# Expert tokens gathered from DRAM by indirect DMA, instead of one-hot products

## The chip, the cores and the metric

The kernel runs on one core of a Trainium2 chip. The metric is device time in microseconds (us). Before the change the median of three runs is 2654.95 us (2649.46 to 2660.77).

## The reference

Two layers of a hybrid network over 512 tokens (256 context, 256 latent; the second layer's output is needed for the latent 256 alone). Each layer has four token mixers, an output projection, a second RMSNorm and a mixture of experts. The change lies in the last two. Cut to what matters:

```python
def hier_moe(h, p):                       # h: the tokens after the second norm
    g_sel = argmax(h @ w_router_g + b_router_g)          # 1 of 4 groups
    top_v, top_i = lax.top_k(e_logits[rows, g_sel], 2)   # 2 of its 8 experts
    weights = softmax(top_v) * g_w
    ...
    # each expert: its tokens' rows, silu(rows @ w_gate) * (rows @ w_up) @ w_down,
    # added to the token with the token's weight
```

An expert has three fp32 matrices: gate and up of 1024x512, down of 512x1024. There are 32 experts in a layer, and all of their weights are read in each layer: 192 MiB. Every token goes to two of them.

## The kernel before

**The second norm.** `tail` (L1597) takes the token tiles of 128 one by one: `project` forms the output projection and adds it to the residual `x`, `norm2` (L1407) makes the normed rows `h2` on VectorE, transposes them on TensorE (8 transposes of 128x128 fp32, L1426) for the router's product, and `split3` (L1432) splits them into three bfloat16 parts whose sum is the fp32 row: the tile `h2p`, 128 partitions by 3 parts by `nt` token tiles by 1024, which stays in SBUF. `nt` is 4 in layer 0 and 2 in layer 1. ScalarE and, by turns, VectorE and GpSimd do the split. `route` (L1439) then makes, for each token and expert, its position in the expert's list (`posm`, -1 where it isn't routed there) and its weight, again as three bfloat16 parts (`wt3`).

**A pair of experts.** `moe` (L1636) goes through 16 pairs. For each, `pair` (L1524) has 128 places, 64 for either expert. `onehot` (L1517) compares `posm` with 0 to 63 on VectorE: a bfloat16 matrix of tokens by places with a 1 where a token holds a place. The expert's tokens, transposed, come from products of `h2p` with it: 8 blocks of 128 features, `nt` token tiles and 3 parts each, summed in PSUM (tile `pg`) and copied to `xT` by ScalarE. Products of the one-hot with the weights give each place's weight (`pw`, `ws`); a transpose of the one-hot (`pT`, `oT`) brings results back to tokens. Then the gate and the up product (`pgate`, `pup`: 32 matmul records each, two experts in two halves of the columns), the activation (`hd`), four transposes (`ph`), the down product (`pd`), the weighting (`yp`, two parts), and the products `py` with `oT`, which add to `x`: the left half of the features on VectorE, the right half by way of ScalarE (`ta`, three buffers) and GpSimd.

**Weights.** `eload` (L1666) brings the weights in tiles of 1 MiB, 12 for a pair in the order gate, up, down, on SyncE's queue. They go round a ring of slots: `EB` (L25) says how many lie on the left and on the right of SBUF in each layer, and four more are the buffers of the output projection's weights. That is 4 + 5 + 4 = 13 slots in layer 0 and 6 + 5 + 4 = 15 in layer 1. The left ones are opened (L1856) and filled before `tail`, the right ones (L1873) as soon as the buffers below them come free. A load into a slot waits on SyncE's queue until the product that read the slot's former tile is done.

**Order.** The kernel is written with a tile framework that lists each engine's instructions in an order of its own making when the program is built, by what it supposes to be ready; at run time each engine keeps that order. So the one-hot products of the next pair stand between the other matmuls of this one, in places that differ from pair to pair. An expert with over 64 tokens would go through `overflow` (L1701), a loop at run time that calls `pair` once more; the counts of the matmul records (1024 for `pgate`, 32 for each of 32 pairs) show that it has no turn here.

Of the kernel before, what the change touches and what calls it, by code (L numbers as in the profile page):

```python
# [9 lines left out]
F32 = mybir.dt.float32  # L10
BF = mybir.dt.bfloat16
F32R = mybir.dt.float32r
I32 = mybir.dt.int32
AF = mybir.ActivationFunctionType
OP = mybir.AluOpType
AX = mybir.AxisListType
# [4 lines left out]
D = 1024  # L21
T = 512
EPS = 1e-6
GN_EPS = 64e-5
EB = ((4, 5), (6, 5))  # L25
CDEC = math.exp(-0.5)
NEG = -1e30

# [9 lines left out]
C_SLT = C_MG + 128  # L38
C_MA = C_SLT + 128
C_ROPE = C_MA + 256  # L40
C_END = C_ROPE + 128

P_N1, P_N2, P_MU, P_W0, P_A0, P_KK, P_KA, P_RK, P_LNG = 0, 8, 16, 24, 28, 32, 34, 36, 38
P_AB, P_GLN, P_BGLU = 40, 42, 44
# [3 lines left out]
def _consts():  # L48
    c = np.zeros((128, C_END), np.float32)
    p = np.arange(128)  # L50
    c[:, C_ID:C_ID + 128] = np.eye(128)
    s = p % 64
    t = np.arange(64)
    c[:, C_MRW:C_MRW + 64] = s[:, None] < t
    c[:, C_MRW + 64:C_MRW + 128] = s[:, None] <= t
    c[:, C_MG:C_MG + 64] = s[:, None] <= t
    c[:, C_MG + 64:C_MG + 128] = s[:, None] >= t
    q = np.arange(128)
    c[:, C_MA:C_MA + 128] = np.where(q[None, :] <= p[:, None], 0.0, NEG)
    c[:, C_MA + 128:C_MA + 256] = np.where(q[None, :] >= p[:, None], 0.0, NEG)  # L60
    c[:, C_BLK:C_BLK + 128] = (p[:, None] // 64) == (p[None, :] // 64)
    tok = np.arange(256, dtype=np.float32)
    inv = np.float32(10000.0) ** (-np.arange(16, dtype=np.float32) / np.float32(16))
    ang = np.concatenate([np.floor(tok / 64)[:, None] * inv, (tok % 64)[:, None] * inv], axis=1)
    ang = ang.astype(np.float32)
    c[:, C_ROPE:C_ROPE + 64] = np.cos(ang).reshape(2, 128, 32).transpose(1, 0, 2).reshape(128, 64)
    c[:, C_ROPE + 64:C_ROPE + 128] = np.sin(ang).reshape(2, 128, 32).transpose(1, 0, 2).reshape(128, 64)

    r = p % 32
    c[:, C_SEL:C_SEL + 12 * L] = r[:, None] == np.arange(12 * L)  # L70
    c[:, C_SLT:C_SLT + 128] = p[:, None] < p[None, :]
    c[:, C_IO:C_IO + 64] = np.arange(64)

    un = p[:, None] % 4 * 4 + np.arange(4)[None, :]
    c[:, C_UN:C_UN + 64] = (un[:, :, None] == np.arange(16)).reshape(128, 64)

    c[:, C_MK:C_MK + 4] = s[:, None] // 16 == np.arange(4)
    return c
# [97 lines left out]
class Net:  # L176
# [1227 lines left out]
            self.tt(xo, xo, tm, OP.add, self.nc.gpsimd if n else None)  # L1404


    def norm2(self, t, x, rw, lo, h2p, wr, lg, pool):  # L1407

        nc = self.nc
        V, G = nc.vector, nc.gpsimd  # L1410
        s, tl = t // 2, t - lo // 128
        xs = x[t]
        y = self.rstd([xs], pool, "n2", 2)
        h2 = pool.tile([128, D], F32, tag="h2", bufs=2, name="h2")
        for n in range(2):
            self.bt = f"B{n}"
            cs = slice(512 * n, 512 * n + 512)
            self.stt(h2[:, cs], xs[:, cs], y, self.bcast(rw, 40 + s, n), OP.mult, OP.mult)
            self.tt(h2[:, cs], self.bcast(rw, 6 + s, n), h2[:, cs], OP.add)
        hT = pool.tile([128, 8, 128], F32, tag="h2T", bufs=1, name="h2T")  # L1420
        for kb in range(2):
            self.bt = f"B{kb}"
            ps = self.pb()
            for k in range(4):
                c = 512 * kb + 128 * k
                nc.tensor.transpose(ps[:, 128 * k:128 * k + 128], h2[:, c:c + 128], self.ident)  # L1426
            (V.tensor_copy if kb else nc.scalar.copy)(hT[:, 4 * kb:4 * kb + 4, :].rearrange("p k n -> p (k n)"), ps)
        for k in range(8):
            self.mm(lg[:, 36 * tl:36 * tl + 36], hT[:, k, :], wr[:, k, :], k == 0, k == 7)
        self.split3([h2p[:, i, tl, :] for i in range(3)], h2, G if t % 2 else V)  # L1430

    def split3(self, o, r, eng):  # L1432

# [87 lines left out]
                    self.cst[:, None, C_IO:C_IO + 64].to_broadcast([128, nt, 64]), OP.is_equal)  # L1521
        return p

    def pair(self, wts, posv, wtv, h2p, x, mb, lo, pool, pooled=(1, 1, 1, 1)):  # L1524

        nc = self.nc
        V, G = nc.vector, nc.gpsimd
        nt = (512 - lo) // 128
        wg, wu, wd = wts
        p = self.onehot(posv, nt, pool, "oh", 2)  # L1530
        pf = p.rearrange("p t e n -> p t (e n)")
        xT = pool.tile([128, 8, 128], F32, tag="xT", bufs=2, name="xT")
        for kb in range(2):
            ps = self.bank("G", "pg")
            for kk in range(4):
                k = 4 * kb + kk
                for t in range(nt):
                    for i in range(3):
                        self.mm(ps[:, 128 * kk:128 * kk + 128], h2p[:, i, t, 128 * k:128 * k + 128], pf[:, t, :],
                                t == 0 and i == 0, t == nt - 1 and i == 2)  # L1540
            self.act(xT[:, 4 * kb:4 * kb + 4, :].rearrange("p k n -> p (k n)"), ps, AF.Copy)
        pT = self.bank("C", "pT", BF)
        for t in range(nt):
            nc.tensor.transpose(pT[:, 128 * t:128 * t + 128], pf[:, t, :], self.identb)
        oT = pool.tile([128, nt, 128], F32R, tag="oT", bufs=2, name="oT")
        V.tensor_copy(oT.rearrange("p t n -> p (t n)"), pT[:, 0:128 * nt])
        pw = self.pc("pw")
        for t in range(nt):
            self.mm(pw[:, 0:6], pf[:, t, :], wtv[:, t], t == 0, t == nt - 1)
        ws = pool.tile([128, 1], F32, tag="ws", bufs=2, name="ws")  # L1550
        for e in range(2):
            r = slice(64 * e, 64 * e + 64)
            V.tensor_reduce(ws[r], pw[r, 3 * e:3 * e + 3], AX.X, OP.add)
        pg, pu = self.pa("pgate"), self.pa("pup")
        for ps, w in ((pg, wg), (pu, wu)):
            for k in range(8):
# [40 lines left out]
    def tail(self, l, lo, acc, rm, w):  # L1597
# [4 lines left out]
        st["posm"] = posm = rm.tile([128, nt, 32], F32, name="posm")  # L1602
        st["wt3"] = wt3 = rm.tile([128, nt, 32, 3], BF, name="wt3")
        st["cnt"] = cnt = rm.tile([128, 32], F32, name="cnt")
        st["h2p"] = h2p = rm.tile([128, 3, nt, D], BF, name="h2p")
        nb = 4 * nt
        st["plan"] = plan = rm.tile([1, nb + 1], I32, name="plan")
        st["base"] = base = rm.tile([128, nb], F32, name="base")
# [1 line left out]
        with self.tc.tile_pool(name=f"rt{l}", bufs=1, reuse_waits="tile") as rp:  # L1610
            wr = rp.tile([128, 8, 36], F32, name="wr")
            nc.scalar.dma_start(wr, io["w_r"][l])
            bs = [None, None]
            for s in range(lo // 256, 2):
                bs[s] = rp.tile([128, D], F32, name=f"bs{s}")
                for n in range(2):
                    self.bt = f"B{n}"
                    cs = slice(512 * n, 512 * n + 512)
                    ps = self.pb("bs")
                    self.mm(ps, self.sel[l][:, 4 + s:5 + s].to_broadcast([128, 128]), self.mods[:, cs], True, True)  # L1620
                    self.act(bs[s][:, cs], ps, AF.Copy, scale=0.5)
            rw = self.rows(l, rp)
            lg = self.pc("lg")
            for t in range(lo // 128, 4):
                self.project(t, w, acc, x, bs, lo, rp)
                self.norm2(t, x, rw, lo, h2p, wr, lg, rp)
            for s in range(lo // 256, 2):
                mb[s] = rm.tile([128, D], F32, name=f"mb{s}")
                for n in range(2):
                    self.bt = f"B{n}"  # L1630
                    self.act(mb[s][:, 512 * n:512 * n + 512], self.bcast(rw, 10 + s, n), AF.Copy)
            self.bt = "B0"
            self.route(l, lg, lo, posm, wt3, cnt, rp)
        return st

    def moe(self, l, lo, st):  # L1636
        nc, io, x = self.nc, self.io, self.x
        posm, wt3, h2p, mb, plan, base = (st[n] for n in ("posm", "wt3", "h2p", "mb", "plan", "base"))
        banks = self.psum(f"pm{l}", G=2, A=2, B=2, C=2)
        self.bt = "B"  # L1640
        with self.tc.tile_pool(name=f"ep{l}", bufs=1, reuse_waits="tile") as ep:
            for q in range(16):
                e0 = 2 * q
                wg, wu, wd = [[self.blocks([self.eload(l, 12 * q + 4 * i + 2 * h + e) for h in range(2)])
                               for e in range(2)] for i in range(3)]
                posv = [posm[:, :, e0 + e:e0 + e + 1] for e in range(2)]
                wtv = wt3[:, :, e0:e0 + 2, :].rearrange("p t e i -> p t (e i)")
                self.pair((wg, wu, wd), posv, wtv, h2p, x, mb, lo, ep, (1, q < 15, 1, q < 15))
                if q == 0:
                    self.overplan(lo, st["cnt"], plan, base, ep)  # L1650
            self.overflow(l, x, mb, lo, posm, wt3, plan, base, h2p, ep)
        banks.__exit__(None, None, None)

    def eopen(self, l, side, bufs):
# [43 lines left out]
        self.tsc(be, be, 31.0, OP.min)  # L1698
        V.tensor_copy(plan[:, 1:nb + 1], be[0:1])

    def overflow(self, l, x, mb, lo, posm, wt3, plan, base, h2p, pool):  # L1701

        nc, tc, io = self.nc, self.tc, self.io
        V = nc.vector
# [4 lines left out]
        with tc.For_i(0, nv, 1) as b:  # L1709
# [13 lines left out]
            wv = pool.tile([128, nt, 2, 3], BF, name="owv")  # L1723
            for i in range(2):
                V.tensor_copy(wv[:, :, i, :], wt3[:, :, bass.ds(e, 1), :].rearrange("p t o i -> p t (o i)"))
            self.pair(w, [pe[:, i] for i in range(2)], wv.rearrange("p t e i -> p t (e i)"), h2p, x, mb, lo, pool)

    def final(self, x, out, pool):
        nc = self.nc
# [171 lines left out]
```

## Time and profile before

| what | value |
|---|---|
| median of 3 runs | 2654.95 us |
| the profiled execution's own time | 2654.23 us |
| its span, first to last instruction | 2652.4 us |
| granted TensorE clock, mean | 0.934 |
| layer 0, expert stage, mark of the first to the last pair | 915.39 to 1465.61 us |
| layer 1, expert stage, mark of the first to the last pair | 2160.06 to 2625.09 us |

All steps are worked out against the profiled execution's 2654.23 us; 1.8 us of it lie outside the span. A pair's mark is the start of VectorE's product of the activation with the up product (`hd<-hd,pup`), of which every pair has one; the distance of two marks is a pair's whole period. A busy share says how full an engine was, not that it set the pace; who waited for whom says that.

### The profile page before, as it was taken

How to read it: one execution, taken by the hardware profiler on the slowest of the kernel's cores; microseconds unless marked ns; L12 is line 12 of the kernel's file. 1: busy time of each engine (PE TensorE's matmuls, PEld its weight loads, DVE VectorE, ACT ScalarE, POOL GpSimd, SP SyncE). 2: the span in 40 equal slices, each digit the busy share in tenths (PEclk: the TensorE clock that was granted, in tenths of full speed). 3: DMA queues.
4: the chain of work that ended last, by engine and by line, in shares of the span. 5: the costliest groups of instructions: out<-in, count | busy, mean ns of one | idle time of the engine just before them, and what ended most of it. 6: DMA issues, size and time to landing. Idle time of an engine off the chain costs nothing. (4 is left out here: it accounts for less than half of the span.)

```text
span 2652.4 us, 42883 instructions
## 1 busy us (share of the span) xinstructions
PE 2417.8 (91%) x17431; PEld 1464.8 (55%) x17431; DVE 1156.0 (44%) x3013; ACT 660.0 (25%) x1163; POOL 705.8 (27%) x601
## 2 busy tenths in 40 slices
PE   5879989999999899999999797998989989999997
PEld 4757756666764444444443576666768644333332
DVE  6586466474214343222222667657573342122212
ACT  2232543222212111111111313343223211111111
POOL 2223411123431033322332323342224311111121
PEclk8887988999999899999999787887989989999999
DMA  6332111123560699788888233312124579999994
GB/s 220 114 113 89 60 38 36 45 60 111 180 236 18 265 391 370 306 319 340 322 316 336 72 129 113 116 65 82 56 81 147 213 316 419 411 394 399 399 402 171
DMA packets 143693, 548.25 MB, mean 207 GB/s; under 512 B 35028, under 2 KB 66132, under 8 KB 93060
## 3 DMA queue, kind: packets, MB, share of 16 engines
q1 hardware_dynamic: 138224, 539.51, 54.0%
q10 hardware_dynamic: 5268, 5.94, 0.7%
q8 instruction: 141, 2.31, 0.3%
q14 instruction: 60, 0.49, 0.1%
HBM read 541.78 MB, written 3.60 MB: 206 GB/s over the span
## 5 line engine op out<-in xcount | busy, mean ns | idle before, releaser
L270 PE MATMUL pa<-hh,gs 128*128 128x512 f32 (+2 forms) x1440 | 439.4, 378 | 12.6 <-ACT sg L273 5.2
L276 POOL TENSOR_TENSOR gs<-g,gs 128x1024 fp32r<-128x1024 f32 (+1 forms) x106 | 255.5, 2414 | 548.5 <-PE pa L270 214.5
L276 POOL TENSOR_TENSOR ta<-ta,mb 128x512 f32<-128x512 f32 x93 | 127.9, 1382 | 835.4 <-ACT ta L273 835.4
L270 PEld LDWEIGHTS pa<-hh,gs 128*128 128x128 f32 (+1 forms) x1440 | 264.7, 197 | 76.8 <-issue 18.4
L270 PE MATMUL pd<-w,hT 128*64 128x512 f32 x1024 | 276.6, 599 | 13.1 <-ACT hT L273 11.9
L270 PE MATMUL pa<-hl,gs 128*128 128x512 f32 (+2 forms) x720 | 263.9, 378 | 0.0
L270 PE MATMUL pgate<-w,xT 128*64 128x512 f32 x1024 | 251.5, 597 | 0.0
L270 PE MATMUL pup<-w,xT 128*64 128x512 f32 x1024 | 249.2, 594 | 0.0
L270 PEld LDWEIGHTS <-h2p 128*128 128x128 bf16 x2304 | 134.8, 99 | 78.0 <-issue 72.5
L273 ACT ACTIVATE gs<-g 128x1024 fp32r<-128x1024 f32 (+1 forms) x106 | 110.5, 1045 | 245.7 <-PE pa L270 172.4
L270 PE MATMUL pg<-oh,h2p 128*128 128x128 bf16 x2304 | 163.2, 223 | 5.9 <-DVE nv L1680 4.2
L270 PEld LDWEIGHTS pd<-w,hT 128*64 128x64 f32 x1024 | 81.5, 136 | 146.7 <-issue 124.6
L270 PEld LDWEIGHTS pa<-hl,gs 128*128 128x128 f32 (+1 forms) x720 | 143.9, 200 | 30.4 <-issue 11.5
L270 PEld LDWEIGHTS pup<-w,xT 128*64 128x64 f32 x1024 | 78.3, 137 | 143.1 <-issue 139.3
L270 PEld LDWEIGHTS pgate<-w,xT 128*64 128x64 f32 x1024 | 74.8, 137 | 139.8 <-issue 129.2
L270 PE MATMUL py<-yp,oT 128*128 128x512 f32 x384 | 133.3, 441 | 10.9 <-ACT ta L273 5.0
L286 DVE SCALAR_TENSOR_TENSOR hd<-hd,pgate 128x512 f32<-128x512 f32 x32 | 22.0, 688 | 246.6 <-ACT hd L273 246.6
L276 POOL TENSOR_TENSOR x<-x,ta 128x512 f32<-128x512 f32 x93 | 121.6, 1315 | 4.9
L270 PE MATMUL pa<-gs,hh 128*128 128x256 f32 x480 | 111.0, 327 | 6.9 <-POOL gs L276 6.7
L276 DVE TENSOR_TENSOR hd<-hd,pup 128x512 f32<-128x512 f32 x32 | 22.0, 688 | 217.9 <-PE pup L270 217.9
L286 DVE SCALAR_TENSOR_TENSOR yp<-pd,ws,yp 128x512 fp32r<-128x512 f32 x64 | 47.8, 746 | 152.6 <-ACT yp L273 152.6
L273 ACT ACTIVATE yp<-pd,ws 128x512 fp32r<-128x512 f32 x64 | 44.1, 688 | 272.9 <-PE pd L270 272.9
(504 smaller groups left out, 3744.7 us busy)
## 6 DMA issues: line engine op xcount, KB each, us to landing
w<-in_w_g SPq DMA_DIRECT2D x128, 1024.0 KB, 8.0
w<-in_w_d SPq DMA_DIRECT2D x128, 1024.0 KB, 10.6
w<-in_w_u SPq DMA_DIRECT2D x128, 1024.0 KB, 8.6
g<-in_w_ada SPq DMA_DIRECT2D x96, 512.0 KB, 3.7
g<-in_w_in_gate SPq DMA_DIRECT2D x64, 512.0 KB, 3.6
g<-in_w_in_rwkv SPq DMA_DIRECT2D x16, 512.0 KB, 3.5
wb<-in_w_branch SPq DMA_DIRECT2D x64, 128.0 KB, 2.7
w<-in_w_out SPq DMA_DIRECT2D x8, 1024.0 KB, 6.2
```

The lines of the kernel that those rows point to most:

```text
L270: self.nc.tensor.matmul(out, lhsT, rhs, start=start, stop=stop, skip_group_check=True)
L273: self.nc.scalar.activation(out, in_, f, **kw)
L276: (eng or self.nc.vector).tensor_tensor(out, a, b, op)
L286: self.nc.vector.scalar_tensor_tensor(out, a, s, b, op0=op0, op1=op1)
```

## The change

The second norm writes each tile of normed rows, in fp32, to a buffer in DRAM (`h2d`), on SyncE's queue; `h2p` and its split go. `pair` is cut in three. `seek` makes the one-hot, multiplies it with three columns (the row number in its tile, the tile's offset less 1024, and 1) to get for each place the number of its token, or 1024 for an empty place, and with the weights as before; then GpSimd issues an indirect DMA that fetches the row of each place from DRAM into one of three tiles `xg`, and skips numbers past the end. `bring` clears the empty places by multiplying `xg` with the third column, transposes it by 8 transposes of 128x128 fp32 and copies it to `xT`; it also makes `oT`. `pair` keeps the rest. Pair q requests the rows of pair q + 2 before its own products and brings those of pair q + 1 after them. The space of `h2p` goes in part to weight slots: 7 + 5 + 4 in layer 0 and 7 + 5 + 4 in layer 1.

```diff
-EB = ((4, 5), (6, 5))
+EB = ((4, 7), (7, 5))
...
+    c[:, C_ROW] = p
...
     def norm2(...):
+        nc.sync.dma_start(h2d[128 * tl:128 * tl + 128], h2)
...
-        self.split3([h2p[:, i, tl, :] for i in range(3)], h2, G if t % 2 else V)
...
+    def seek(self, posv, wtv, h2d, lo, pool):
...
+        p = self.onehot(posv, nt, pool, "oh", 3)
+        pf = p.rearrange("p t e n -> p t (e n)")
+        pw = self.pc("pw")
+        for t in range(nt):
+            self.mm(pw[:, 8:11], pf[:, t, :], self.tid[:, t], t == 0, t == nt - 1)
+        for t in range(nt):
+            self.mm(pw[:, 0:6], pf[:, t, :], wtv[:, t], t == 0, t == nt - 1)
...
+        V.tensor_copy(at[:, 0:3], pw[:, 8:11])
+        self.stt(ix, at[:, 0:1], 1024.0, at[:, 1:2], OP.add, OP.add)
...
+        xg = self.xg[self.xi % 3]
+        self.xi += 1
+        nc.gpsimd.indirect_dma_start(xg, None, h2d, bass.IndirectOffsetOnAxis(ap=ix, axis=0),
+                                     bounds_check=128 * nt - 1, oob_is_err=False)
+        return pf, at, ws, xg
+
+    def bring(self, sent, lo, pool):
...
+        self.tsc(xg, xg, at[:, 2:3], OP.mult)
         for kb in range(2):
             ps = self.bank("G", "pg")
             for kk in range(4):
                 k = 4 * kb + kk
-                for t in range(nt):
-                    for i in range(3):
-                        self.mm(ps[:, 128 * kk:128 * kk + 128], h2p[:, i, t, 128 * k:128 * k + 128], pf[:, t, :],
-                                t == 0 and i == 0, t == nt - 1 and i == 2)
+                nc.tensor.transpose(ps[:, 128 * kk:128 * kk + 128], xg[:, 128 * k:128 * k + 128], self.ident)
             self.act(xT[:, 4 * kb:4 * kb + 4, :].rearrange("p k n -> p (k n)"), ps, AF.Copy)
...
     def moe(self, l, lo, st):
...
+            self.xg = [ep.tile([128, D], F32, name=f"xg{i}") for i in range(3)]
+            for xg in self.xg:
+                nc.gpsimd.memset(xg, 0.0)
...
+            sent = seek(0), seek(1)
+            got = self.bring(sent[0], lo, ep)
             for q in range(16):
...
+                sent = sent[1], seek(q + 2)
+                self.pair((wg, wu, wd), got, x, mb, lo, ep, (1, q < 15, 1, q < 15))
+                if q < 15:
+                    got = self.bring(sent[0], lo, ep)
```

## Rows read from the trace of the kernel before

**Rows 1.** The page's busy time: engine, us (share of the span), instructions.

```profile
PE 2417.8 (91%) x17431; PEld 1464.8 (55%) x17431; DVE 1156.0 (44%) x3013; ACT 660.0 (25%) x1163; POOL 705.8 (27%) x601
```

**Rows 2.** Stretches, one of layer 0 and two of layer 1.

```profile
core 0: us, PE busy (x) PEld busy (x) DVE busy (x) ACT busy (x) POOL busy (x), PEclk, DMA share, GB/s
1300.00:1350.00 50.00, 48.52 (x266) 20.13 (x265) 14.89 (x26) 8.44 (x14) 19.34 (x15) 1.00 0.83 320
...
2200.00:2250.00 50.00, 49.23 (x331) 22.51 (x332) 15.22 (x22) 9.41 (x16) 10.82 (x8) 1.00 1.01 419
...
2400.00:2450.00 50.00, 47.16 (x240) 17.78 (x237) 9.97 (x21) 7.82 (x13) 5.20 (x4) 1.00 0.98 401
```

**Rows 3.** Waits in layer 1, SyncE's queue and TensorE: total us, times, longest.

```profile
SPq L224 <- PE pgate L270: 181.0, 47, 29.2
...
PE pd L270 <- DMA w<-in_w_u: 0.6, 1, 0.6
```

**Rows 4.** Timeline of VectorE, layer 0: marks of pairs 1, 2, 11, 12, 15, 16.

```profile
915.39 0.69 DVE L276 TENSOR_TENSOR hd<-hd,pup 128x512 f32<-128x512 f32 x1 [5.49 <-PE pup L270]
...
947.70 0.69 DVE L276 TENSOR_TENSOR hd<-hd,pup 128x512 f32<-128x512 f32 x1 [4.56 <-PE pup L270]
...
1284.65 0.69 DVE L276 TENSOR_TENSOR hd<-hd,pup 128x512 f32<-128x512 f32 x1 [9.81 <-PE pup L270]
...
1323.27 0.69 DVE L276 TENSOR_TENSOR hd<-hd,pup 128x512 f32<-128x512 f32 x1 [7.86 <-PE pup L270]
...
1432.81 0.69 DVE L276 TENSOR_TENSOR hd<-hd,pup 128x512 f32<-128x512 f32 x1 [5.55 <-PE pup L270]
...
1465.61 0.69 DVE L276 TENSOR_TENSOR hd<-hd,pup 128x512 f32<-128x512 f32 x1 [5.55 <-PE pup L270]
```

**Rows 5.** Timeline of VectorE, layer 1: marks of pairs 1, 9, 10, 15, 16.

```profile
2160.06 0.69 DVE L276 TENSOR_TENSOR hd<-hd,pup 128x512 f32<-128x512 f32 x1 [5.49 <-PE pup L270]
...
2407.62 0.69 DVE L276 TENSOR_TENSOR hd<-hd,pup 128x512 f32<-128x512 f32 x1 [5.55 <-PE pup L270]
...
2439.37 0.69 DVE L276 TENSOR_TENSOR hd<-hd,pup 128x512 f32<-128x512 f32 x1 [5.55 <-PE pup L270]
...
2595.75 0.69 DVE L276 TENSOR_TENSOR hd<-hd,pup 128x512 f32<-128x512 f32 x1 [5.55 <-PE pup L270]
...
2625.09 0.69 DVE L276 TENSOR_TENSOR hd<-hd,pup 128x512 f32<-128x512 f32 x1 [5.55 <-PE pup L270]
```

**Rows 6.** Timeline of TensorE in layer 0, one-hot products inside the up product.

```profile
1077.77 1.07 PE L270 MATMUL pup<-w,xT 128*64 128x512 f32 x2
1078.77 4.86 PE L270 MATMUL pg<-oh,h2p 128*128 128x128 bf16 x84
1083.57 7.08 PE L270 MATMUL pup<-w,xT 128*64 128x512 f32 x30
```

**Rows 7.** Timeline of TensorE: the second norm's transposes, and products with the weights.

```profile
840.05 1.25 PE L1426 MATMUL pb<-cst,h 128*128 128x128 f32 x8 [0.39 <-DVE h L276]
...
901.19 0.24 PE L270 MATMUL pw<-wt,oh 128*128 128x6 bf16 x4
```

**Rows 8.** Instructions on the tile h2p, VectorE: ns min/median/max, first and last start.

```profile
L276 DVE TENSOR_TENSOR h<-h,h2p x3: 1215/1215/1216, 822.6 to 2108.8; 128x1024 f32<-128x1024 f32 x3
```

**Rows 9.** Timeline of TensorE, head of layer 0's expert stage.

```profile
894.31 6.82 PE L270 MATMUL pg<-oh,h2p 128*128 128x128 bf16 x96 [2.32 <-DVE nv L1680]
...
901.36 7.09 PE L270 MATMUL pgate<-w,xT 128*64 128x512 f32 x32
```

**Rows 10.** Timeline of SyncE's queue: first loads into freed slots, and the last ones.

```profile
905.04 3.76 SPq L224 DMA_DIRECT2D w<-in_w_g  x3
...
2149.71 0.33 SPq L224 DMA_DIRECT2D w<-in_w_g  x1
...
2592.31 10.69 SPq L224 DMA_DIRECT2D w<-in_w_d  x4
```

**Rows 11.** DMA issues: count, KB each, median us from issue to landing.

```profile
w<-in_w_d SPq DMA_DIRECT2D x128, 1024.0 KB, 10.6
...
wr<-in_w_r ACTq DMA_DIRECT2D x2, 144.0 KB, 4.8
```

More of the change, by code (lines that the diff above doesn't have):

```diff
@@ L40 @@
 C_ROPE = C_MA + 256
-C_END = C_ROPE + 128
+C_ROW = C_ROPE + 128
+C_END = C_ROW + 1
 P_N1, P_N2, P_MU, P_W0, P_A0, P_KK, P_KA, P_RK, P_LNG = 0, 8, 16, 24, 28, 32, 34, 36, 38
@@ L1404, in project, with norm2 @@
             self.tt(xo, xo, tm, OP.add, self.nc.gpsimd if n else None)
-    def norm2(self, t, x, rw, lo, h2p, wr, lg, pool):
+    def norm2(self, t, x, rw, lo, h2d, wr, lg, pool):
         nc = self.nc
-        V, G = nc.vector, nc.gpsimd
+        V = nc.vector
         s, tl = t // 2, t - lo // 128
@@ L1522, in onehot @@
         return p
-    def pair(self, wts, posv, wtv, h2p, x, mb, lo, pool, pooled=(1, 1, 1, 1)):
+    def seek(self, posv, wtv, h2d, lo, pool):
         nc = self.nc
-        V, G = nc.vector, nc.gpsimd
+        V = nc.vector
         nt = (512 - lo) // 128
-        wg, wu, wd = wts
-        p = self.onehot(posv, nt, pool, "oh", 2)
+        p = self.onehot(posv, nt, pool, "oh", 3)
         pf = p.rearrange("p t e n -> p t (e n)")
+        pw = self.pc("pw")
[3 more added lines that the diff above has]
+            self.mm(pw[:, 0:6], pf[:, t, :], wtv[:, t], t == 0, t == nt - 1)
+        ix = pool.tile([128, 1], I32, tag="ix", bufs=3, name="ix")
+        at = pool.tile([128, 4], F32, tag="at", bufs=3, name="at")
+        V.tensor_copy(at[:, 0:3], pw[:, 8:11])
+        self.stt(ix, at[:, 0:1], 1024.0, at[:, 1:2], OP.add, OP.add)
+        ws = at[:, 3:4]
+        for e in range(2):
+            r = slice(64 * e, 64 * e + 64)
+            V.tensor_reduce(ws[r], pw[r, 3 * e:3 * e + 3], AX.X, OP.add)
+        xg = self.xg[self.xi % 3]
[4 more added lines that the diff above has]
+    def bring(self, sent, lo, pool):
+        nc = self.nc
+        nt = (512 - lo) // 128
+        pf, at, ws, xg = sent
+        self.tsc(xg, xg, at[:, 2:3], OP.mult)
         xT = pool.tile([128, 8, 128], F32, tag="xT", bufs=2, name="xT")
@@ L1545, in pair @@
         oT = pool.tile([128, nt, 128], F32R, tag="oT", bufs=2, name="oT")
[L1546 to L1553, printed above, removed]
+        nc.vector.tensor_copy(oT.rearrange("p t n -> p (t n)"), pT[:, 0:128 * nt])
+        return xT, oT, ws
+    def pair(self, wts, got, x, mb, lo, pool, pooled=(1, 1, 1, 1)):
+        nc = self.nc
+        G = nc.gpsimd
+        nt = (512 - lo) // 128
+        wg, wu, wd = wts
+        xT, oT, ws = got
         pg, pu = self.pa("pgate"), self.pa("pup")
@@ L1604, in tail @@
         st["cnt"] = cnt = rm.tile([128, 32], F32, name="cnt")
-        st["h2p"] = h2p = rm.tile([128, 3, nt, D], BF, name="h2p")
+        st["h2d"] = h2d = self.dr.tile([128 * nt, D], F32, name=f"h2d{l}")
         nb = 4 * nt
@@ L1625, in tail @@
                 self.project(t, w, acc, x, bs, lo, rp)
-                self.norm2(t, x, rw, lo, h2p, wr, lg, rp)
+                self.norm2(t, x, rw, lo, h2d, wr, lg, rp)
             for s in range(lo // 256, 2):
@@ L1637, in moe @@
         nc, io, x = self.nc, self.io, self.x
-        posm, wt3, h2p, mb, plan, base = (st[n] for n in ("posm", "wt3", "h2p", "mb", "plan", "base"))
+        posm, wt3, h2d, mb, plan, base = (st[n] for n in ("posm", "wt3", "h2d", "mb", "plan", "base"))
         banks = self.psum(f"pm{l}", G=2, A=2, B=2, C=2)
@@ L1641, in moe, with seek @@
         with self.tc.tile_pool(name=f"ep{l}", bufs=1, reuse_waits="tile") as ep:
+            nt = (512 - lo) // 128
+            self.tid = ep.tile([128, nt, 3], BF, name="tid")
+            nc.gpsimd.memset(self.tid[:, :, 2:3], 1.0)
+            for t in range(nt):
+                nc.gpsimd.memset(self.tid[:, t, 1:2], 128.0 * t - 1024.0)
+            nc.vector.tensor_copy(self.tid[:, :, 0:1], self.const(C_ROW, 1, ep)[:, None, :].to_broadcast([128, nt, 1]))
+            self.xg = [ep.tile([128, D], F32, name=f"xg{i}") for i in range(3)]
+            self.xi = 0
+            for xg in self.xg:
+                nc.gpsimd.memset(xg, 0.0)
+            def seek(q):
+                if q > 15:
+                    return None
+                posv = [posm[:, :, 2 * q + e:2 * q + e + 1] for e in range(2)]
+                wtv = wt3[:, :, 2 * q:2 * q + 2, :].rearrange("p t e i -> p t (e i)")
+                return self.seek(posv, wtv, h2d, lo, ep)
+            sent = seek(0), seek(1)
+            got = self.bring(sent[0], lo, ep)
             for q in range(16):
-                e0 = 2 * q
                 wg, wu, wd = [[self.blocks([self.eload(l, 12 * q + 4 * i + 2 * h + e) for h in range(2)])
                                for e in range(2)] for i in range(3)]
-                posv = [posm[:, :, e0 + e:e0 + e + 1] for e in range(2)]
-                wtv = wt3[:, :, e0:e0 + 2, :].rearrange("p t e i -> p t (e i)")
-                self.pair((wg, wu, wd), posv, wtv, h2p, x, mb, lo, ep, (1, q < 15, 1, q < 15))
+                sent = sent[1], seek(q + 2)
+                self.pair((wg, wu, wd), got, x, mb, lo, ep, (1, q < 15, 1, q < 15))
+                if q < 15:
+                    got = self.bring(sent[0], lo, ep)
                 if q == 0:
                     self.overplan(lo, st["cnt"], plan, base, ep)
-            self.overflow(l, x, mb, lo, posm, wt3, plan, base, h2p, ep)
+            self.overflow(l, x, mb, lo, posm, wt3, plan, base, h2d, ep)
         banks.__exit__(None, None, None)
@@ L1699, in overplan, with overflow @@
         V.tensor_copy(plan[:, 1:nb + 1], be[0:1])
-    def overflow(self, l, x, mb, lo, posm, wt3, plan, base, h2p, pool):
+    def overflow(self, l, x, mb, lo, posm, wt3, plan, base, h2d, pool):
         nc, tc, io = self.nc, self.tc, self.io
@@ L1725, in overflow @@
                 V.tensor_copy(wv[:, :, i, :], wt3[:, :, bass.ds(e, 1), :].rearrange("p t o i -> p t (o i)"))
-            self.pair(w, [pe[:, i] for i in range(2)], wv.rearrange("p t e i -> p t (e i)"), h2p, x, mb, lo, pool)
+            sent = self.seek([pe[:, i] for i in range(2)], wv.rearrange("p t e i -> p t (e i)"), h2d, lo, pool)
+            self.pair(w, self.bring(sent, lo, pool), x, mb, lo, pool)
     def final(self, x, out, pool):
```

## Prediction

> **What bounds the kernel now.** I read the page's busy table first, then the stages, then single pairs of experts. TensorE is busy 91% of the span [rows 1], but that is an average over stages with different limits, and the change touches two of them: the two mixture-of-experts stages, one per layer, each 16 pairs of experts long. In a stretch of the first (layer 0, 512 tokens) TensorE is full at the granted clock 1.00 (2.4 GHz) while the DMA engines are busy 0.83 of the time at 320 GB/s; in the second (layer 1, 256 tokens) the DMA engines are at 0.98 to 1.01 and 401 to 419 GB/s [rows 2]. So layer 0 looks bound by TensorE. Layer 1 is less plain. The waits say that SyncE's queue, which issues every weight load, waits for the gate products that free a slot, and that TensorE's one listed wait for a weight there is 0.6 us [rows 3]. Also the mark that I use for a pair (VectorE multiplying by the up product, once per pair) comes at an even 31.75 us in mid-stage [rows 5]; a queue that was late would jitter. Layer 1 is thus TensorE-bound with a weight stream that has almost no room left. In layer 0 the marks lie 32.3 us apart for the first pair, 38.6 us in the middle, and 32.8 us for the last, where no one-hot product is left to do [rows 4].
>
> **The change, part by part.** Sums are against the profiled execution, 2654.2 us (span 2652.4), 0.7 us under the median of the three runs.
>
> *Removed: one-hot products.* A pair does 8 blocks x 3 parts x 4 token tiles = 96 of them in layer 0 and 48 in layer 1. Inside a run of 84, from its first to the next instruction, 4.80 us pass: 57 ns each [rows 6]. That is 5.5 us per pair in layer 0 and 2.7 us in layer 1. They stand on the path because nothing else is idle on TensorE meanwhile. Between the first and the last mark lie 15 intervals: 550.2 us in layer 0, 465.0 us in layer 1 [rows 4, 5]. Taken out: 15 x 5.5 = 82 us, and 15 x 2.7 = 41 us.
>
> *Added on TensorE.* Eight fp32 transposes of 128x128 per pair; the second norm already does eight such, in 1.25 us [rows 7]. Products with the token-number column, 4 or 2 per pair; the like products with the weights take 0.24 us for four [rows 7]. Together 1.5 us per pair in layer 0 and 1.4 us in layer 1: 22 and 21 us. The products with the weights and the one-hot transposes only move.
>
> *Added beside it.* VectorE scales the gathered rows: 128x1024 fp32, nearest row 1.2 us [rows 8], plus small copies; it is busy 10 to 15 us in 50 there [rows 2], so this hides, and without that cover it would cost 1.5 us a pair. GpSimd issues 32 gathers. The trace of before shows no gather, so bounds: nothing, up to some 30 us of GpSimd each before the next pair needs it (it is busy 5 to 19 us in 50 [rows 2], and a gather has over one pair of time). Its in-order queue holds each gather until the index is there, and behind it wait the previous pair's scaling and adding to x, whose three buffers give that some slack. I take zero in mid-stage.
>
> *Rows through DRAM.* Six writes of 512 KiB go into SyncE's queue, where each holds the weight loads behind it until its tile is normed. The first pair's weights wait for earlier buffers in that stretch anyway, so zero; bound, one norm step of some 10 us in each layer if a load needed at once stands behind. The split into three bfloat16 parts goes (1.2 us VectorE operations and their like on ScalarE and GpSimd [rows 8]); it lies beside the output projection's matmuls: zero, at most 0.5 us gained at the last tile.
>
> *The head of each stage.* Before, one-hot products follow the one-hot at once, and the first gate product starts 7.1 us later in layer 0 (894.31 to 901.36) [rows 9]. Now the chain is: index product, two small VectorE operations, gather, scale, transposes, copy. Nearest row for the gather: a 144 KB load on a hardware queue, 4.8 us to landing; a 1 MB weight load, 10.6 us behind others [rows 11]. With 1 us for the index, 1.2 us for the scale, 1.3 us for the transposes and 0.6 us for the copy the chain is 9 to 15 us instead of 7. Below I cannot see a gain, as the gather must land; above I allow 15 us per layer, since three 128x1024 clears on GpSimd also stand ahead of it. I take +4 us per layer, by the nearest row. The Trainium skill, "DMA: Bandwidth & Descriptors", section "Anatomy of one DMA", gives about 2.0 us plus bytes over 436 GB/s for a transfer of this kind, an estimate of 2.6 us for 64 rows; by it the head would cost 2 us less. No run here shows it.
>
> *Weight slots.* 13 become 16 in layer 0 and 15 become 16 in layer 1: 3 MiB and 1 MiB load ahead, when the DMA engines have room. In layer 0 this hides; in layer 1 it shortens the stream.
>
> **The sum.** Layer 0: 550.2 - 82 + 22 = 490 us, a gain of 60, less 4 for the head: 56. The stream must hold this. It runs from the first freed slot at 905.04 [rows 10] and must carry 176 MiB of weights and 1024 rows of 4 KiB, 188.7 MB; the rate at a full share is 401/0.98 = 409 GB/s [rows 2], so 461 us, which is earlier than TensorE needs it. Layer 1: TensorE alone would give 465 - 41 + 21 = 445 us. The stream now carries 176 MiB and 512 rows, 186.6 MB: 456 us from 2149.71, ending at 2606, where before its last loads were issued up to 2603 and landed some 10 us later [rows 10, 11]. The last down product needs them just after the last mark, so the marks span 446 us at best. Two limits so close add up their waits: I take 452 us, a gain of 13, less 4: 9. Together 65 us: **2654.2 - 65 = 2589, say 2590.**
>
> **The rivals.**
>
> *A: lost lead-ins.* The order of TensorE's instructions is fixed when the program is built. In the middle of layer 0 two up products, then one-hot products, then thirty: the two alone take 1.0 us where streaming takes 0.23 each [rows 6]. If the transposes fall into such places, they cost more than their own time. From the last pair, which has no one-hot product: 32.8 + 1.5 + 1.0 = 35.3 us for 12 intervals and 32.3 - 5.5 + 1.5 = 28.3 us for three: 509 us, a gain of 41; in layer 1 likewise 29.3 + 1.4 + 1.0 = 31.7 us, no gain but about 7 us in the first three. Less 8 for the heads: 2614. For it: the 38.6 us intervals. Against: the index products leave the down products, which removes one break.
>
> *B: the break-free order throughout.* All layer 0 intervals at 28.3 us; then the stream binds at 461 us from 909: mark span 447 us, gain 103; layer 1 gains 19; less 8: 2540. Only the first three pairs show it, with prefetched weights.
>
> *C: the gathers slow the weight stream (slower).* They share the 16 engines. With rate r, layer 0 ends its stream at 909 + 188.7/r and layer 1 at 2154 + 186.6/r; against the last marks of before, 1465.6 and 2625.1, the sum turns into a loss below 365 GB/s. At 350 GB/s it is 2698. Against: 4 MiB and 2 MiB beside 176; at a full share even the slowest of the stretches makes 320/0.83 = 386 GB/s [rows 2]. The skill's same page, "Latency and other measured facts", offers as a best guess that descriptor rings written by GpSimd slow two of the engines; its section "Measured" puts a core's share of HBM at 358 GB/s when its neighbour streams too, which would make this 2674. The trace disagrees with the latter on this lone core: 419 GB/s [rows 2].
>
> *D: the request ahead does not cover.* If a gather took more than a pair's time on GpSimd, every pair would wait; each 4 us of wait in 30 pairs is 120 us: about 2709. The trace says nothing for it but that GpSimd is in order.
>
> *E: a long head*, 15 us per layer: 2612.
>
> **How the numbers follow.** Forecast 0.52, A 0.22, B 0.10, C 0.06, D 0.04, E 0.06. The forecast's own bounds (stream at 401 to 419 GB/s, heads 0 to 15 us, breaks at 0 to 1 us) give 2565 to 2625; the range goes on to 2550 towards B and to 2636 towards a heavier A. Half a per cent, 13 us, is what a measurement here can tell from no change. Faster 0.85 (forecast, B, E and most of A), same 0.05 (A with breaks in every pair), slower 0.10 (C and D).
>
> **What would show it.** Marks 32 to 34 us apart in mid-layer 0 and 30.5 to 31.5 us in mid-layer 1; DMA share above 0.95 in both stages; first gate product about 4 us later after the one-hot; about 82 us less one-hot work in layer 0. Wrong if marks in layer 1 grow past 31.75 us, if TensorE's waits name the gathered tile in mid-stage, or if GB/s at a full share drops below 390.

## The result, and the profile after

The changed kernel takes 2756.97 us (median of 4 runs, 2746.07 to 2767.29) against 2652.2 us (median of 4) for the kernel before on the same chip: a ratio of 1.0402 (95% interval 1.0371 to 1.0432). It is 4% slower, where 2590 us and a gain were forecast. The profiled execution took 2765.96 us, with a span of 2764.2 us, 111.8 us longer than before.

The first fence is from the page of the changed kernel: the span, four engines, two of its costliest groups and the queue of the gathers.

```profile
span 2764.2 us, 39223 instructions
PE 2382.4 (86%) x15479; PEld 1392.6 (50%) x15479; DVE 1191.0 (43%) x3105; ACT 644.8 (23%) x1151; POOL 729.0 (26%) x641
...
q0 software_dynamic: 4608, 6.30, 0.7%
...
L1564 PE MATMUL pg<-cst,xg 128*128 128x128 f32 x256 | 58.8, 379 | 113.6 <-DVE xg L283 113.6
...
L283 DVE TENSOR_SCALAR xg<-xg,at 128x1024 f32<-128x1024 f32 x32 | 27.3, 852 | 253.5 <-DMA xg<-h2d,ix 253.5
```

TensorE was busy 91% before [rows 1] and is at 86% now, although the one-hot products are gone. The transposes of the fetched rows (L1564) work for 58.8 us and keep TensorE idle for 113.6 us, all of it behind the scaling of those rows on VectorE (L283), and the scaling itself waits for the gather. The gathers are small: 6.30 MB and 0.7% of the DMA engines' time.

The waits of the changed kernel, whole span (engine, line, released by whom, us in total, times, longest):

```profile
PE pg L1564 <- DVE xg L283: 113.6, 26, 6.0
...
DVE xg L283 <- DMA xg<-h2d,ix: 253.5, 32, 11.1
```

Thus TensorE was held 26 times, by up to 6.0 us. Before, in layer 1, it waited 0.6 us for a weight [rows 3], and its products with the rows waited once for the one-hot, 0.9 us:

```profile
PE pg L270 <- DVE oh L276: 0.9, 1, 0.9
```

The windows answer to [rows 2]; the same stretches of the changed kernel:

```profile
core 0: us, PE busy (x) PEld busy (x) DVE busy (x) ACT busy (x) POOL busy (x), PEclk, DMA share, GB/s
1300.00:1350.00 50.00, 43.09 (x182) 16.34 (x181) 15.83 (x22) 7.57 (x13) 11.31 (x9) 0.97 0.85 327
2400.00:2450.00 50.00, 40.85 (x167) 14.49 (x165) 9.88 (x20) 7.22 (x12) 6.36 (x5) 0.93 0.85 337
```

In layer 1 the stream fell from 401 GB/s at a share of 0.98 to 337 GB/s at 0.85: it has room that nobody asks for. Now the marks, which answer to [rows 4, 5]; first and last mark of each layer in the changed kernel, with duration and start:

```profile
L278 DVE TENSOR_TENSOR hd<-hd,pup x1: 686/686/686, 920.2 to 920.2; 128x512 f32<-128x512 f32 x1
...
L278 DVE TENSOR_TENSOR hd<-hd,pup x1: 689/689/689, 1488.3 to 1488.3; 128x512 f32<-128x512 f32 x1
...
L278 DVE TENSOR_TENSOR hd<-hd,pup x1: 686/686/686, 2190.4 to 2190.4; 128x512 f32<-128x512 f32 x1
...
L278 DVE TENSOR_TENSOR hd<-hd,pup x1: 687/687/687, 2735.5 to 2735.5; 128x512 f32<-128x512 f32 x1
```

The 111.8 us lie as follows: 4.8 up to the first mark of layer 0 (920.2 against 915.39); 17.8 in layer 0's marks (568.0 us against 550.2); 7.7 between layer 0's last mark and layer 1's first; 80.1 in layer 1's marks (545.1 against 465.0); 1.4 behind the last. A mid-stage interval is now about 40 us in both layers, where it had been 38.6 and 31.75.

What a pair looks like is in the timeline of the changed kernel, layer 1 (start, us, engine, line, operation; in brackets the idle time before it and who ended it):

```profile
2485.49 0.20 PE L272 MATMUL pw<-tid,oh 128*128 128x3 bf16 x2
...
2495.92 0.15 DVE L1541 COPY at<-pw 128x3 f32<-128x3 f32 x1
...
2496.65 1.24 DVE L288 SCALAR_TENSOR_TENSOR ix<-at 128x1 int32<-128x1 f32 x1
...
2496.95 7.08 PE L272 MATMUL pgate<-w,xT 128*64 128x512 f32 x30
...
2500.60 1.03 POOL L1549 DMA_INDIRECT xg<-h2d,ix  x1
...
2509.00 0.75 DVE L283 TENSOR_SCALAR xg<-xg,at 128x1024 f32<-128x1024 f32 x1 [10.87 <-DMA xg<-h2d,ix]
...
2509.80 0.48 PE L1564 MATMUL pg<-cst,xg 128*128 128x128 f32 x1 [5.77 <-DVE xg L283]
2510.21 1.97 PE L272 MATMUL pup<-w,xT 128*64 128x512 f32 x2
2512.11 1.76 PE L1564 MATMUL pg<-cst,xg 128*128 128x128 f32 x7
2513.80 8.13 PE L272 MATMUL pup<-w,xT 128*64 128x512 f32 x30
```

The gather at 2500.60 is the request for the pair after next, as the change says. But its scaling and its transposes have come forward with it: they stand right behind this pair's gate product, and their own gate product is that of two pairs on, which starts at 2573.25, some 63 us behind them. The framework's order puts them where it supposes the rows to be ready, and two xT buffers let it. So the request is two pairs ahead of the product, and 8.4 us ahead of the scaling on which the transposes wait. TensorE keeps its order, idles 5.77 us, and then runs slower: two up products take 1.97 us where the timeline of before had 1.07 [rows 6], and the transposes 379 ns on average (first fence), 421 ns in the median, where 273 ns is the median in a faster kernel below. The request itself was late too: its index product was done at 2485.7, but VectorE turned to it only at 2495.92, behind output work of the pair before, and GpSimd, behind such work too, issued it at 2500.60.

### The profile page after: what moved, and what is told of

Read it like the earlier page. It is cut to its first block, busy times and chain, and to the rows that moved or that the text cites. A ratio compares the mean times of both kernels' runs of the same rounds, so it can differ in the third digit from the quotient of the medians.

```text
span 2764.2 us, 39223 instructions
## 1 busy us (share of the span) xinstructions
PE 2382.4 (86%) x15479; PEld 1392.6 (50%) x15479; DVE 1191.0 (43%) x3105; ACT 644.8 (23%) x1151; POOL 729.0 (26%) x641
## 5 line engine op out<-in xcount | busy, mean ns | idle before, releaser
L272 PE MATMUL pup<-w,xT 128*64 128x512 f32 x1024 | 284.0, 639 | 0.0
L272 PE MATMUL pd<-w,hT 128*64 128x512 f32 x1024 | 265.9, 599 | 15.6 <-ACT hT L275 15.2
L272 PE MATMUL pgate<-w,xT 128*64 128x512 f32 x1024 | 264.8, 606 | 0.0
L272 PEld LDWEIGHTS pd<-w,hT 128*64 128x64 f32 x1024 | 89.3, 137 | 152.9 <-issue 131.2
L1564 PE MATMUL pg<-cst,xg 128*128 128x128 f32 x256 | 58.8, 379 | 113.6 <-DVE xg L283 113.6
L283 DVE TENSOR_SCALAR xg<-xg,at 128x1024 f32<-128x1024 f32 x32 | 27.3, 852 | 253.5 <-DMA xg<-h2d,ix 253.5
L275 ACT ACTIVATE xT<-pg 128x512 f32<-128x512 f32 x64 | 35.4, 595 | 401.2 <-PE pup L272 332.9
L1564 PEld LDWEIGHTS pg<-cst,xg 128*128 128x128 f32 x256 | 41.8, 192 | 167.5 <-DVE xg L283 133.6
L272 PEld LDWEIGHTS py<-yp,oT 128*128 128x128 f32 x384 | 61.1, 188 | 125.5 <-ACT ta L275 47.2
L288 DVE SCALAR_TENSOR_TENSOR yp<-pd,at,yp 128x512 fp32r<-128x512 f32 x64 | 47.8, 747 | 177.2 <-ACT yp L275 177.2
```

Of the source, the lines that this page charges most:

```text
L272: self.nc.tensor.matmul(out, lhsT, rhs, start=start, stop=stop, skip_group_check=True)
L275: self.nc.scalar.activation(out, in_, f, **kw)
L283: e.tensor_scalar(out, a, s1, None, op0=op0)
L288: self.nc.vector.scalar_tensor_tensor(out, a, s, b, op0=op0, op1=op1)
L1564: nc.tensor.transpose(ps[:, 128 * kk:128 * kk + 128], xg[:, 128 * k:128 * k + 128], self.ident)
```

## Experiments

Four theories stood at first. **W**: TensorE waits for the rows because the order brought their use forward. **S**: the gathers slow the weight stream. **V**: VectorE, held by the gather, is late with the pair's activation. **O**: the break of transposes in the up product costs by itself. The kernel before, in that set of runs, took 2655.74 us (7 runs).

**One xT buffer.** With one, the transposes of a later pair cannot overtake this pair's up product.

```diff
-        xT = pool.tile([128, 8, 128], F32, tag="xT", bufs=2, name="xT")
+        xT = pool.tile([128, 8, 128], F32, tag="xT", bufs=1, name="xT")
```

> Edit: one buffer instead of two for the transposed rows xT, so that the next pair's copy, and with it the transposes two pairs ahead, cannot run before this pair's up product is done. In the list of TensorE's instructions the transposes then stand behind the up product, not between gate and up. Theory W (the consumer of a gather stands right behind its own request, and TensorE waits there in order and comes back at a lower clock): TensorE's waits for the gathered tile fall from 114 us to under 15, marks about 34 us apart in mid-layer 0 and 32 in mid-layer 1, time 2757 - 114 - about 26 x 1.5 of slow clock = 2605, between 2580 and 2630. Rival S (gathers and row writes slow the weight stream): the marks stay at 38 to 41 us, time 2740 or more. Rival O (only the place of the transposes inside the up product costs): the waits stay, time about 2757 - 26 x 2 = 2705.

Measured: 2585.15 us, ratio 0.9716 (0.9677 to 0.9755); span 2584.6 us, marks spanning 495.8 us in layer 0 and 437.6 in layer 1, 33.64 and 29.75 us apart in mid-stage (34 and 32 had been expected). One number in the source turns 4% slower into 2.8% faster. First the two windows of this kernel:

```profile
1300.00:1350.00 50.00, 46.16 (x197) 17.00 (x197) 19.54 (x31) 9.08 (x16) 22.43 (x18) 1.00 0.91 369
2400.00:2450.00 50.00, 47.71 (x213) 17.41 (x210) 12.06 (x23) 7.82 (x13) 7.73 (x7) 1.00 1.01 419
```

Its waits, of TensorE and of VectorE:

```profile
PE pg L1564 <- DVE xg L283: 13.2, 4, 4.6
...
DVE xg L283 <- DMA xg<-h2d,ix: 262.4, 32, 11.3
```

And its timeline, in layer 1, from a request to the first transposes that use it:

```profile
2369.30 1.03 POOL L1549 DMA_INDIRECT xg<-h2d,ix  x1
...
2372.14 7.45 PE L272 MATMUL pup<-w,xT 128*64 128x512 f32 x31
...
2377.99 0.76 DVE L283 TENSOR_SCALAR xg<-xg,at 128x1024 f32<-128x1024 f32 x1 [11.16 <-DMA xg<-h2d,ix]
2378.78 0.69 DVE L288 SCALAR_TENSOR_TENSOR hd<-hd,pgate 128x512 f32<-128x512 f32 x1
2379.63 0.69 DVE L278 TENSOR_TENSOR hd<-hd,pup 128x512 f32<-128x512 f32 x1 [0.17 <-PE pup L272]
2380.34 0.44 PE L1564 MATMUL pg<-cst,xg 128*128 128x128 f32 x2 [0.75 <-ACT xT L275]
```

The gather still lands 8 us after its issue and VectorE still waits for it, 262.4 us in all. But the up product runs on TensorE meanwhile, and the activation is ready when the up product is (0.17 us of idle time). TensorE's wait is gone but for 13.2 us in four places. The clock is at 1.00 in both windows, and the stream at 419 GB/s at a share of 1.01 with all the gathers in it. So S falls, and so does V. W fits; O is not excluded, as the transposes have left the up product too: they now fill the gap in which TensorE would wait for the activation.

**Requests a pair earlier.** `seek(q + 3)`, four buffers for the rows and all that goes with them, and one slot less in either layer's ring to make room; two xT buffers as in the change.

```diff
-EB = ((4, 7), (7, 5))
+EB = ((4, 6), (6, 5))
...
-                sent = sent[1], seek(q + 2)
+                sent = sent[1], sent[2], seek(q + 3)
```

> Edit: rows requested three pairs ahead, with four tiles for them, and one weight slot fewer in either layer to make room. Theory W: each request has one pair more before its consumer, the waits fall under 15 us, and the time is that of the kernel with one xT buffer, 2580 to 2630. Rival S: unchanged at 2740 or more, as every byte still moves. Rival O: about 2705.

Measured: 2581.88 us, ratio 0.9731 (0.9691 to 0.977); marks spanning 493.7 and 439.1 us. Here the order came out as with one xT buffer, transposes behind the up product. So this run confirms the gain and tells no more of the cause than the one before it: what changed was again the place, and not how long the rows had been there (VectorE waits 239.4 us for gathers).

**Transposes that read no rows.** The eight transposes read a constant tile in place of the gathered one, so the experts' rows are left out of the products; gathers and scaling stay. The ring has one slot less in either layer.

```diff
-EB = ((4, 7), (7, 5))
+EB = ((4, 6), (6, 5))
...
-                nc.tensor.transpose(ps[:, 128 * kk:128 * kk + 128], xg[:, 128 * k:128 * k + 128], self.ident)
+                nc.tensor.transpose(ps[:, 128 * kk:128 * kk + 128], self.xz[:, 128 * k:128 * k + 128], self.ident)
```

> Edit: the transposes read a constant tile, so the expert products no longer use the gathered rows; requests, gathers and their scaling on VectorE are all kept, and one weight slot fewer in either layer makes room. Theory W: TensorE waits for no gather, 2580 to 2630, although the same bytes move. Rival S: 2740 or more. A third rival, V (VectorE's own wait for the gather holds the activation behind it): VectorE still waits some 250 us for gathers and the time stays above 2690.

Measured: 2577.68 us (2 runs), ratio 0.9701 (0.9677 to 0.9724); marks spanning 499.6 and 440.0 us. All the traffic is there, and in the waits VectorE's for it:

```profile
DVE xg L283 <- DMA xg<-h2d,ix: 274.8, 32, 12.0
```

This kernel does all the work of the change without TensorE's dependence on a gather, and it is as fast as the two above: those have nothing left to win from the gather's time. Its transposes, too, stand behind the up product, so it says nothing of O.

**The slots of before.** Only the ring goes back to its former size. In the changed kernel it has 4 + 7 + 4 = 15 slots in layer 0 and 7 + 5 + 4 = 16 in layer 1 (the section on the change and the prediction say 16 for both).

```diff
-EB = ((4, 7), (7, 5))
+EB = ((4, 5), (6, 5))
```

> Edit: the changed kernel with the weight slots of before (4 + 5 + 4 and 6 + 5 + 4), all else kept. Theory W: TensorE waits for no weights, so the slots do not matter: 2757 within 12 us. Rival: the larger ring had its part in the loss (loads further ahead crowd the gathers, whose landing is 8 us): landing falls by 1 us or more and the time by 20 us or more.

Measured: 2774.26 us, ratio 1.0436 (1.0401 to 1.0472), which overlaps the changed kernel's interval. The time is 17 us above the changed kernel's, where the expectation allowed 12; each against its own runs of the kernel before, 9 us are left. Its waits show much the same:

```profile
PE pg L1564 <- DVE xg L283: 116.0, 27, 6.1
```

So the slots are no part of the loss that can be measured, and the next two kernels could do with fewer.

**The break without the wait, and with it.** W and O had not been told apart. Two kernels now hold the transposes between gate and up product by force, with three xT and four row buffers, and have the same order on TensorE in mid-stage. They differ in when a row is asked for. `behind` is the last gate product; the up products are queued behind the last transpose in the same way, and the scaling behind the last addition of the pair before on VectorE. In both:

```diff
+                with self.tc.issue_after(behind.ins) if behind is not None else ExitStack():
+                    tr = nc.tensor.transpose(ps[:, 128 * kk:128 * kk + 128], xg[:, 128 * k:128 * k + 128], self.ident)
```

The kernel with the early request, where also the last additions of a pair are queued behind the request, so that it goes out:

```diff
-            sent = seek(0), seek(1)
+            sent = seek(0), seek(1), seek(2), seek(3)
...
-                sent = sent[1], seek(q + 2)
+                sent = sent[1], sent[2], sent[3], seek(q + 4)
```

The one with the late request keeps the two lines of the change, and queues the copy of the index behind the last product on VectorE of the pair before:

```diff
+        with self.tc.issue_after(self.vm.ins) if self.vm is not None else ExitStack():
+            V.tensor_copy(at[:, 0:3], pw[:, 8:11])
```

> The eight transposes of pair q+2 are held on TensorE between pair q's gate and up products, as in the changed kernel, but their rows are requested two pairs before that place instead of some 8 us before it, and the scaling stands behind the pair's last addition on VectorE, so that they have landed. Three xT buffers, four row buffers, ring slots 4+5 and 6+4. If what costs the time is TensorE's wait for rows (the wait), TensorE shows next to no idle time ended by the scaling, the granted clock in mid-stage is back near 1.00, pairs take about 33.7 us in layer 0 and 29.8 us in layer 1, and the run takes 2570 to 2610 us. If the break between gate and up product costs by itself (the break), because float32 transposes between two long products lower the clock or refill the weights, the pairs stay near 40 us and the run takes 2690 us or more, with no wait to show for it.

> The same kernel as the one before with the same order on TensorE in mid-stage and the same buffers, but the rows are requested late, in the tail of the pair before the one behind whose gate product they are transposed, as in the changed kernel. The wait: TensorE idles 4 to 6 us per pair behind the scaling, the clock falls to 0.90 to 0.97, pairs take about 40 us, and the run takes 2730 to 2800 us, some 150 us more than the one before it. The break: no more than 20 us apart from the one before it, both slow.

Measured, beside 2650.41 us for the kernel before (7 runs): with the early request 2593.0 us, ratio 0.9772 (0.9741 to 0.9803); with the late one 2774.81 us, ratio 1.0473 (1.0443 to 1.0503). TensorE's wait for rows in the first:

```profile
PE pg L1566 <- DVE xg L283: 4.0, 3, 1.8
```

A window of it in layer 1:

```profile
2400.00:2450.00 50.00, 47.02 (x202) 16.85 (x202) 16.20 (x26) 8.40 (x14) 13.61 (x10) 1.00 1.01 415
```

Its transposes in the tile view (duration in ns: least, median, most):

```profile
L1566 PE MATMUL pg<-cst,xg x256: 272/273/477, 898.7 to 2500.0; 128*128 128x128 f32 x128
```

And its timeline in layer 1, where gate product, transposes and up product follow one another without idle time:

```profile
2434.81 7.08 PE L272 MATMUL pgate<-w,xT 128*64 128x512 f32 x30
2441.82 1.09 PE L1566 MATMUL pg<-cst,xg 128*128 128x128 f32 x8
2442.85 7.09 PE L272 MATMUL pup<-w,xT 128*64 128x512 f32 x32
```

Of the second kernel, the busy engines of its page:

```profile
PE 2355.6 (85%) x15479; PEld 1384.8 (50%) x15479; DVE 1196.9 (43%) x3105; ACT 646.1 (23%) x1151; POOL 730.5 (26%) x643
```

TensorE's wait for rows in it:

```profile
PE pg L1567 <- DVE xg L283: 134.0, 28, 10.2
```

The same window:

```profile
2400.00:2450.00 50.00, 40.03 (x162) 15.14 (x162) 10.31 (x19) 6.15 (x10) 6.36 (x5) 0.88 0.78 303
```

And its timeline there, from a request to the up product:

```profile
2430.49 1.03 POOL L1550 DMA_INDIRECT xg<-h2d,ix  x1
...
2438.95 0.75 DVE L283 TENSOR_SCALAR xg<-xg,at 128x1024 f32<-128x1024 f32 x1 [10.46 <-DMA xg<-h2d,ix]
...
2439.75 1.97 PE L1567 MATMUL pg<-cst,xg 128*128 128x128 f32 x8 [5.81 <-DVE xg L283]
2441.65 7.68 PE L272 MATMUL pup<-w,xT 128*64 128x512 f32 x32
```

In mid-stage the early kernel issues a gather 58 us (layer 1) or 67 us (layer 0) before its scaling, the late one some 8 us. The break alone costs little: pairs take 34.13 and 30.65 us, against 33.64 and 29.75 with one xT buffer, half a microsecond to a whole one, and the transposes take 1.09 us for eight. The wait costs 173.8 us of span (2764.7 against 2590.9). Of it 130.0 us are TensorE's idle time behind the scaling (134.0 less 4.0), and 47.1 us are the same 15479 matmuls taking longer (2355.6 against 2308.5 us busy on the page of the early one). The two make 177.1; the 3 us too many went out of other gaps. Of the 47.1 us, 43.3 lie right behind the wait: 14.5 in the transposes (53.0 us against 38.5) and 28.8 in the up products, while the gate products, which stand ahead of it, take the same (265.3 and 265.1 us). The up products, the early kernel first:

```profile
L272 PE MATMUL pup<-w,xT 128*64 128x512 f32 x1024 | 230.0, 595 | 0.0
...
L272 PE MATMUL pup<-w,xT 128*64 128x512 f32 x1024 | 258.8, 657 | 0.0
```

O falls as a cause, W stands.

The kernels with one xT buffer and with earlier requests beat both the kernel before and the changed one, by 2.8% and 2.7% of the former; their intervals do not tell which of them is better.

## Why the prediction was wrong

**The step that failed** is in "Added beside it": "a gather has over one pair of time", and "I take zero in mid-stage". I read "two pairs ahead" from the place of the call in the source, and asked whether GpSimd could issue in time. I did not ask where the consumer would stand. My own account of the kernel before says that the framework makes each engine's order by what it supposes to be ready, and that one-hot products of the next pair stand among this pair's matmuls; the transposes that replace them were free to do the same, a pair further forward. What the runs put in the place of zero: 113.6 us of idle TensorE, and slower matmuls behind it. Against the kernel with one xT buffer the span is 179.6 us longer, of which 100.4 us are more idle time there (113.6 less 13.2), 63.0 us are TensorE's busy time (2382.4 against 2319.4 us), and 16 us are other gaps that I did not trace further.

**What held.** With the consumer in a harmless place the total comes out near the forecast: 2585.15 us for 2590. Its terms, read from that kernel: layer 0's marks span 495.8 us for 490; layer 1's 437.6 us for 452. The 445 us that TensorE alone was to need were at least 7 us too many, and the stream's limit of 446 us came from 409 GB/s, where layer 1 of that kernel reaches 419 GB/s, gathers included. So in layer 1 adding up two close limits was too careful by 14 us, and in layer 0 the sum was 6 us too hopeful. Up to the first mark that kernel took 7.6 us more than the kernel before (922.96 against 915.39), and 4.9 us more between the layers, where the heads had been given 4 us each. That the total agrees within 5 us is in part luck: these errors offset one another.

**The heads.** I took 4 us each. Up to the first mark of layer 0 it was 4.8 us, row writes and all; the stretch between the layers, head of layer 1 included, grew by 7.7 us. The timeline of the changed kernel's first head:

```profile
897.38 1.20 POOL L1549 DMA_INDIRECT xg<-h2d,ix  x1 [10.47 <-DVE at L1546]
...
901.47 0.75 DVE L283 TENSOR_SCALAR xg<-xg,at 128x1024 f32<-128x1024 f32 x1 [1.60 <-DMA xg<-h2d,ix]
902.28 1.97 PE L1564 MATMUL pg<-cst,xg 128*128 128x128 f32 x8 [4.57 <-DVE xg L283]
```

The gather took 4.1 us from the start of its issue to the scaling, and the eight transposes, behind 4.57 us of idle time, 1.97 us instead of 1.25 [rows 7]; the granted clock was 0.50 (1.2 GHz) there, from 897 to 906 us, and 1.00 around the eight of that row, from 838 to 846 us. Scaling took 0.75 us, not the 1.2 us of the nearest row. E, the long head, did not come.

**The rivals.** D, "the request ahead does not cover", had the size: 4 us of wait in 30 pairs, 120 us, 2709 us; measured were 113.6 us in 26. It had 0.04, because I tied it to a gather that "took more than a pair's time", and a gather takes 8 us. A rival should be priced by the effect, here that TensorE waits for a gather, with each way in which that could come about. C, the slowed stream, falls: 337 GB/s in the changed kernel is what TensorE asks for, and 419 GB/s flow beside the same gathers as soon as it does not wait. That rate shows no sign of the two slower engines that the Trainium skill, "DMA: Bandwidth & Descriptors", section "Latency and other measured facts", offers as a guess; no run here shows the engines one by one. The prediction sets its 358 GB/s against the 419 GB/s of this trace, but that figure is for two cores that stream at once, and here one core runs alone, so the trace says nothing about it. A had the place of the break right (two up products amid transposes) and its price of about 1 us a pair: 0.5 to 0.9 us measured, there with all eight transposes ahead of the up product. B did not come. The slots, held to shorten layer 1's stream, did nothing that can be measured in the changed kernel.

**The signs.** Two of the three that were to prove the forecast wrong came: marks in layer 1 past 31.75 us, and waits of TensorE that name the gathered tile. I knew what to look for and gave it no term in the sum.

## What to carry to other kernels

A request made ahead only covers as far as its first consumer stays behind: count from the issue of the transfer to the first instruction on a busy in-order engine that needs it, not to the product for which it is meant. Where a framework orders the engines, the number of buffers of the consumer's output can decide how far forward the consumer goes; one buffer less can be the faster choice, as it was here by 6.9 points of the ratio (1.0402 to 0.9716). Put such a consumer where another engine's wait has to be sat out anyway, and price a stall of TensorE above its length, since the matmuls behind it ran slower as well.

## What the runs showed of the hardware

An indirect DMA for the 128 places of a pair holds GpSimd for 1.03 us and lands 3.2 us after its issue at best, 7.9 us in the median. It fetches 48 rows of 4 KiB on average (6.30 MB in 32 gathers; 64 rows in layer 0, 32 in layer 1). The tile view of the changed kernel (duration in ns, least, median, most; then the times to landing):

```profile
L1549 POOL DMA_INDIRECT xg<-h2d,ix x32: 990/1028/1199, 897.4 to 2660.5; - x32
...
DMA to landing us min/median/max: 3.2/7.9/8.6
```

The time goes with how busy the DMA engines are, and not with the bytes. At the head of layer 1, at a DMA share of 0.16 (2168 to 2175 us), the scaling of 32 rows starts 3.3 to 3.4 us after the issue. In mid-stage of that layer, at a share of 0.96 to 1.02, it starts 7.9 to 8.6 us after it; in mid-stage of layer 0, mostly at about 0.77, that of 64 rows starts 7.1 to 7.9 us after it, but for one of 4.4 us.

The Trainium skill, "DMA: Bandwidth & Descriptors", section "Anatomy of one DMA", gives 2.0 us plus bytes over 436 GB/s, an estimate of 2.3 us for 32 rows and 2.6 us for 64; the best gather here, one of 32 rows, took 0.9 us more and the usual one about three times as long, so beside a busy stream the trace disagrees.

The clock was the other thing that I had not priced. In the window 2400 to 2450 us the granted clock is 1.00 (2.4 GHz) with the break alone, and 0.88 on average with the wait, between the two levels of 1.2 and 2.4 GHz; what TensorE did before is in the timelines, where it had stood idle for 5.81 us and the work right behind is slower: 32 up products behind such a wait took 7.68 us instead of 7.09, and eight transposes 1.97 us instead of 1.09. Around that wait, from 2427 to 2433 us, in the gate product, the granted clock is 1.00; in the idle time and the transposes behind it, it falls to 0.50 (1.2 GHz), as the window below shows; from 2444 to 2449 us, in the up product, it is 1.00 again.

```profile
2437.00:2442.00 5.00, 2.25 (x10) 1.86 (x12) 1.35 (x2) 0.84 (x2) 0.00 (x0) 0.50 1.02 426
```
